# Quarter updates of the down products sent by ScalarE and adding transfers, and chunk 1's up in seven products

## The chip, the core and the metric

The kernel runs on one core of one Trainium2 chip. The engines are TensorE (PE in the profile; PEld is its weight load), VectorE (DVE), ScalarE (ACT), GpSimd (POOL) and SyncE (SP). Weights come from HBM over transfers that SP issues. The metric is the device time of one execution in microseconds, the median over runs.

## What is computed

A decoder trunk over 512 tokens of width 1024, two layers deep. A layer is a half-step feed-forward (FFN), a mixer, and a second half-step feed-forward; the first layer's mixer is a gated linear attention (GLA), the second's a stick-breaking attention (SB). A norm ends the whole.

```python
def swiglu(h, w_gate, w_up, w_down):
    return (jax.nn.silu(h @ w_gate) * (h @ w_up)) @ w_down

# layer i
x += 0.5 * swiglu(rmsnorm(x, ffn1_norm[i]), ...)   # width 1024 -> 2816 -> 1024
x += mixer_i(rmsnorm(x, mix_norm[i]))
x += 0.5 * swiglu(rmsnorm(x, ffn2_norm[i]), ...)
```

So the stages in order are FFN1, GLA, FFN2, FFN3, SB, FFN4. All is in 32-bit floats.

## The kernel before

**Layout.** The state x lies in SBUF as eight tiles `xs[0..7]` of 128 features by 512 tokens. Matmuls run on a rounded format, so each operand is split into a high part (a cast by ACT, L538 for weights, L1261 for data) and a low part (a subtraction by DVE, L539 and L1262), and each 128-row product is three matmuls: high by high, low by high, high by low.

**An FFN stage.** The 2816 inner features are 11 chunks of 256, in five groups: chunk 0; chunks 1 to 3; 4 to 6; 7 to 9; 10 (in the last stage 7 and 8, then 9 and 10). For each chunk come a gate product and an up product, whose product is the inner value; when a group's inner values are there, its down product updates x. A plain gate or up is two features (`feat`, L479) of 24 matmuls of 128x512 each. From chunk 2 on, gate and up use a scheme with seven products instead of eight (`FFN.seven`, L1164): the weight block is cut into quarters, the data in two halves of features by two of tokens, and with sums of quarters and sums of data halves 7 x 12 matmuls of 128x256 do the work. The constants are `SEVEN = 2` for gates and `SEVEN_UP = (2, ..., 10)` for ups. The weight sums (`s12` at L1149 and L1150, `s34` at L1155 and L1156) are DVE's, as are the sums of the normed input (`ts`, L1271, split as `th`, `tl`). The third product of each seven (t3 below, on `s34`) needs all of these. The normed input itself is `xn` (L1255), from x and the scale R, which `rstd_wide` makes at L1019 and L1022.

**The downs.** Groups 1, 2 and 3 have their down in seven products too (`seven_down`), in four parts of two output blocks each, or, for a group of two chunks, in two parts of twice that. In a part the products are, in order: a11 into a PSUM tile `ps_w`, which ACT copies to `ps_z` (L843); t1 into `ps_q`; t2 onto `ps_w`; b21 onto `ps_z`; then t3 onto `ps_w`, b22 onto `ps_q` and t4 onto `ps_w`. For three chunks each is 9 matmuls of 128x256 (L825). After t1, t2, b21, t3, b22 and t4 a quarter of an x tile pair (128 features by 256 tokens) gets half of the running sum added: six updates by DVE (`add`, L831). That of t3 goes by a copy `u3` which ACT takes out of `ps_w` (L869), so that t4 need not wait for DVE. t1 and t3 update the same quarter, and t2 and b22.

**What sets the order.** Program order is not the order on the engines. A `Planner` collects all instructions, prices each by engine, shape and kind, and lists them by dependence, time of readiness and due time, once for each engine; PE's order may pull matmuls ahead out of the next 60. The result is a fixed order on each engine, where an instruction waits at the head of its queue. POOL's instructions stay in program order. Transfers are priced by bytes. So an edit in one place shifts the order around it.

**POOL** has little to do: constants, cleared tiles, and the loads `gr` (L1464), `tri`, `lf`, `negm` (L1959) and `fin` (L2008).

Of the kernel before, what the change touches and what calls it, by code (L numbers as in the profile page):

```python
# [11 lines left out]
F32 = mybir.dt.float32  # L12
# [3 lines left out]
AF = mybir.ActivationFunctionType  # L16
ALU = mybir.AluOpType
PSUM = bass.MemoryType.PSUM

P = 128  # L20
# [409 lines left out]
def turns(t):  # L430

    return t.rearrange("p (two n) -> p n two", two=2)


def flat(ps):

    return ps.rearrange("p (n two) -> p two n", two=2)


def pair(t):  # L440

    return t.rearrange("p (two n) -> p two n", two=2)
# [3 lines left out]
def decoder(ctx: ExitStack, tc: tile.TileContext, a: dict, out: bass.AP):  # L446
    nc = tc.nc
# [28 lines left out]
    xs = [xp.tile([P, T], F32, name=f"x{k}") for k in range(KD)]  # L476
# [311 lines left out]
    def seven_down(pool, w, r0, hs, part, n, per):  # L788

        H = T // 2
        W_ = per * P
        lower, upper = (
            Chunk(w[r0 : r0 + 2 * n * P, c : c + W_].rearrange("(f p) c -> p f c", p=P), 2 * n, W_)
            for c in (part * W_, 512 + part * W_)
        )
        lower.few = upper.few = True
        v = {}

        def halves():

            lo, up = (c.load().rearrange("p (c two) d -> p two c d", two=2) for c in (lower, upper))
            return lo[:, 0], lo[:, 1], up[:, 0], up[:, 1]

        def sums_12(_):
            a11, _, a21, a22 = halves()
            s = v["s12"] = pool().tile([P, 2 * n, W_], F32, tag="s", bufs=4, name="s12")
            nc.vector.tensor_tensor(out=s[:, 0:n], in0=a21, in1=a22, op=ALU.add)
            nc.vector.tensor_tensor(out=s[:, n:], in0=s[:, 0:n], in1=a11, op=ALU.subtract)  # L810
            return s

        def sums_34(_):
            a11, a12, a21, _ = halves()
            s = pool().tile([P, 2 * n, W_], F32, tag="s", bufs=4, name="s34")
            nc.vector.tensor_tensor(out=s[:, 0:n], in0=a11, in1=a21, op=ALU.subtract)
            nc.vector.tensor_tensor(out=s[:, n:], in0=a12, in1=v["s12"][:, n:], op=ALU.subtract)
            return s

        def prod(ps, w, k0, m, b, first):  # L820
            for c in range(n):
                bh, bl = (turns(t) for t in hs[c][b])
                wh, wl = (t[:, k0 + c, m * P : (m + 1) * P] for t in w)
                for i, (l_, r_) in enumerate(((wh, bh), (wl, bh), (wh, bl))):
                    nc.tensor.matmul(  # L825
                        ps, l_, r_, start=first and c + i == 0, stop=c == n - 1 and i == 2, skip_group_check=True
                    )

        def add(m, up, col, ps):
            x = pair(xs[part * per + m + 4 * up][:, col * H : col * H + H])  # L830
            nc.vector.scalar_tensor_tensor(out=x, in0=ps, scalar=0.5, in1=x, op0=ALU.mult, op1=ALU.add)  # L831

        def body_1(W):
            a11, s, v["a2"] = W
            ws, zs, qs = [], [], []
            for m in range(per):
                ws.append(psum("ps_w")[:, 0:H])
                prod(ws[m], a11, 0, m, "b11", True)
            for m in range(per):


                zs.append(psum("ps_z")[:, 0:H])
                nc.scalar.copy(zs[m], ws[m])  # L843
            yield

            ps = psum("ps_q")
            for m in range(per):
                qs.append(ps[:, m * H : (m + 1) * H])
                prod(qs[m], s, 0, m, "t1", m == 0)
            for m in range(per):  # L850
                add(m, 1, 1, flat(qs[m]))
            yield
            for m in range(per):
                prod(ws[m], s, n, m, "t2", False)
                add(m, 0, 1, flat(ws[m]))
            yield
            for m in range(per):
                prod(zs[m], v["a2"], 0, m, "b21", False)
                add(m, 0, 0, flat(zs[m]))
            v["w"], v["q"] = ws, qs  # L860
            yield

        def body_2(W):
            (s,) = W
            ws, qs = v["w"], v["q"]
            for m in range(per):
                prod(ws[m], s, 0, m, "t3", False)
                u3 = pool().tile([P, H], F32, tag="c", bufs=1, name="u3")
                nc.scalar.copy(pair(u3), flat(ws[m]))  # L869
                add(m, 1, 1, pair(u3))  # L870
            yield
            for m in range(per):
                prod(qs[m], s, n, m, "b22", False)
            for m in range(per):
                add(m, 0, 1, flat(qs[m]))
            yield
            for m in range(per):
                prod(ws[m], v["a2"], n, m, "t4", False)
                add(m, 1, 0, flat(ws[m]))
            yield  # L880

        units = [
            (lower, lambda t: halves()[0], n, W_),
            (lower, sums_12, 2 * n, W_),
            (lower, lambda t: halves()[1::2], 2 * n, W_),
        ]
        feed.q.append(Entry(units, body_1))
        feed.q.append(Entry([(lower, sums_34, 2 * n, W_)], body_2))

    def back_tok(w, r0, nf, hs, done):  # L890
# [160 lines left out]
    class FFN:  # L1051
# [8 lines left out]
        NORMED, SEVEN, AHEAD = 6, 2, 2  # L1060
        SEEDED = (0,)
        DOWN_SEVEN = (1, 2, 3)
        SEVEN_UP = (2, 3, 4, 5, 6, 7, 8, 9, 10)

        def __init__(self, wg, wu, wd, gi, nxt, first=False, last=False):
            self.gi, self.normed = gi, False
            if last:
                self.GROUPS = self.LAST_GROUPS
            self.after_ffn = bool(phases) and isinstance(phases[-1], FFN)
            self.defer, self.gates, self.first = [], [], None  # L1070
            self.lead = []
            self.hs = [[] for _ in self.GROUPS]
            base, downs = len(feed.q), []
            self.sums_by = 10**6
            for group, (c0, c1) in enumerate(self.GROUPS):
                slots, put = 2 * (c1 - c0), 0
                for i in range(slots):
                    c, f = c0 + i // 2, i % 2
                    if (c, f) == (self.SEVEN, 0):
                        for put in range(self.AHEAD):  # L1080
                            down(*downs[put], late=put == 0)
                        put = self.AHEAD
                    if f == 0:
                        g, u = Chunk(cols(wg, c * 256, 256), KD, 256), Chunk(cols(wu, c * 256, 256), KD, 256)
                    d = self.defer if i == 0 and c == 0 else None
                    f_ = f
                    if first and c == 0:

                        g, u = (Chunk(cols(w, f * P, P), KD, P) for w in (wg, wu))
                        self.lead += [g, u]  # L1090
                        f_ = 0
                    if c >= self.SEVEN:
                        if f == 0:
                            self.sums_by = min(self.sums_by, len(feed.q) - base)
                            self.seven(g)
                    elif c not in self.SEVEN_UP:
                        feat(g, f_, self.evac_g, defer=d)
                    elif f == 0:
                        feat(g, 0, self.evac_g), feat(g, 1, self.evac_g)
                        self.sums_by = min(self.sums_by, len(feed.q) - base)  # L1100
                    if group - 1 in self.DOWN_SEVEN and f == 0 and c == c0:
                        b0, b1 = self.GROUPS[group - 1]
                        per = 2 if b1 - b0 == 2 else 1
                        args = (lambda: self.tp, wd, b0 * 256, self.hs[group - 1])
                        parts = [(*args, part, b1 - b0, per) for part in range(4 // per)]
                        if group + 1 == len(self.GROUPS) and not last:
                            held = parts.pop()
                        for x in parts:
                            seven_down(*x)
                    if c not in self.SEVEN_UP:  # L1110
                        feat(u, f_, lambda ps, h=group: self.evac_u(ps, h), defer=d)
                    elif f == 1:
                        self.seven(u, group)

                    while c >= self.SEVEN and put < min(len(downs), len(downs) * (i + 1) // 3):
                        down(*downs[put])
                        put += 1
# [9 lines left out]
                if group in self.DOWN_SEVEN:  # L1127
                    downs = []
# [10 lines left out]
        def seven(self, ch, group=None):  # L1139
# [4 lines left out]
            H = T // 2  # L1144
# [58 lines left out]
            def body_2(W):  # L1203
# [1 line left out]
                w, q = (v[n][:, 0:H] for n in "wq")  # L1205
                o0, o1 = v["o"]
                prod(w, s, 0, lambda j: self.t_half(2, j), first=False)
                u3 = self.tp.tile([P, H], F32, tag="c", bufs=1, name="u3")
                nc.scalar.copy(pair(u3), flat(w))
                nc.vector.tensor_tensor(out=o1[:, H:T], in0=u3, in1=o1[:, H:T], op=ALU.add)  # L1210
                yield
# [1149 lines left out]
```

## Time and profile before

| what | value |
|---|---|
| median of 3 runs | 1741.15 us (1739.17 to 1742.62) |
| profiled execution | 1741.74 us, its span 1740.0 us |
| granted TensorE clock | 0.999 |
| PE busy | 1729.9 us, 99%, 13206 matmuls |
| DVE busy | 1618.7 us, 93% |
| ACT busy | 1142.1 us, 66% |
| POOL busy | 10.0 us, 24 instructions |
| moved by transfers | 179.35 MB |

Busy time says which engine is full; the chain of waits says which engine the end depended on. The scale R of FFN2 is ready at 554.6 us and that of FFN4 at 1421.5; FFN3 starts near 880, GLA near 317 and SB near 1164 us.

### The profile page before, as it was taken

How to read it: one execution, taken by the hardware profiler on the slowest of the kernel's cores; microseconds unless marked ns; L12 is line 12 of the kernel's file. 1: busy time of each engine (PE TensorE's matmuls, PEld its weight loads, DVE VectorE, ACT ScalarE, POOL GpSimd, SP SyncE). 2: the span in 40 equal slices, each digit the busy share in tenths (PEclk: the TensorE clock that was granted, in tenths of full speed). 3: DMA queues.
4: the chain of work that ended last, by engine and by line, in shares of the span. 5: the costliest groups of instructions: out<-in, count | busy, mean ns of one | idle time of the engine just before them, and what ended most of it. 6: DMA issues, size and time to landing. Idle time of an engine off the chain costs nothing.

```text
span 1740.0 us, 32878 instructions
## 1 busy us (share of the span) xinstructions
PE 1729.9 (99%) x13206; PEld 1633.0 (94%) x13206; DVE 1618.7 (93%) x2856; ACT 1142.1 (66%) x2056; POOL 10.0 (1%) x24
## 2 busy tenths in 40 slices
PE   9999999999999999999999999999999999999998
PEld 8999999988888999999989999999888888999997
DVE  8999999987888999999999999998898669999997
ACT  7666666664656766666677575657889757666655
POOL 0000000100000000000000000000000000000000
PEclk9999999999999999999999999999999999999999
DMA  6433333321223333333233333233222233333422
GB/s 187 134 101 119 104 116 107 97 95 51 73 98 106 115 106 115 101 119 110 92 115 122 108 112 119 89 105 88 62 73 76 72 106 115 110 110 110 122 87 81
DMA packets 209324, 179.35 MB, mean 103 GB/s; under 512 B 4434, under 2 KB 197252, under 8 KB 209172
## 3 DMA queue, kind: packets, MB, share of 16 engines
q1 hardware_dynamic: 208320, 175.91, 32.8%
q8 instruction: 103, 1.69, 0.4%
q0 software_dynamic: 608, 1.05, 0.2%
q14 instruction: 49, 0.40, 0.1%
q10 hardware_dynamic: 244, 0.29, 0.0%
HBM read 175.17 MB, written 2.10 MB: 102 GB/s over the span
## 4 chain that ended last, share of the span: by engine, by line
PE 91%; DVE 7%; ACT 1%; DMA 1%; issue 1%; DVEq 0%; ACTq 0%; SPq 0%
PE ps_w L1164 21%; PE ps_f L479 15%; PE ps_q L1164 10%; PE ps_w L825 10%; PE ps_q L825 5%; PE ps_z L1164 5%; PE ps_t L479 5%; PE ps_b L479 4%; PE ps_d L479 4%; PE ps_z L825 3%; DVE wl L539 2%; PE ps_z L1849 2%; PE ps_oT L1934 1%; PE ps_T L1919 1%; PE ps_bt L479 1%; PE ps_S L479 1%
## 5 line engine op out<-in xcount | busy, mean ns | idle before, releaser
L538 ACT CAST wh<-s 128x1024 fp32r<-128x1024 f32 (+1 forms) x236 | 229.2, 971 | 113.4 <-PE ps_q L1164 28.1
L539 DVE TENSOR_TENSOR wl<-raw,wh 128x1024 fp32r<-128x1024 f32 x241 | 254.1, 1056 | 31.3 <-ACT wh L538 31.1
L539 DVE TENSOR_TENSOR wl<-s,wh 128x1024 fp32r<-128x1024 f32 (+1 forms) x236 | 263.1, 1115 | 1.6 <-ACT wh L538 1.4
L538 ACT CAST wh<-raw 128x1024 fp32r<-128x1024 f32 x241 | 221.3, 921 | 58.5 <-PE ps_b L479 20.7
L1164 PE MATMUL ps_w<-th,wh 128*128 128x256 f32 x864 | 238.0, 275 | 0.0
L1164 PE MATMUL ps_w<-th,wl 128*128 128x256 f32 x864 | 237.6, 275 | 0.0
L1164 PE MATMUL ps_w<-tl,wh 128*128 128x256 f32 x864 | 237.6, 275 | 0.0
L479 PE MATMUL ps_f<-xh,wh 128*128 128x512 f32 x432 | 166.7, 386 | 0.0
L1164 PEld LDWEIGHTS ps_w<-th,wh 128*128 128x128 f32 x864 | 165.8, 192 | 0.4 <-ACT o L1197 0.2
L1164 PEld LDWEIGHTS ps_w<-tl,wh 128*128 128x128 f32 x864 | 165.9, 192 | 0.0
L1164 PEld LDWEIGHTS ps_w<-th,wl 128*128 128x128 f32 x864 | 165.9, 192 | 0.0
L479 PE MATMUL ps_f<-xh,wl 128*128 128x512 f32 x432 | 163.7, 379 | 0.0
L479 PE MATMUL ps_f<-xl,wh 128*128 128x512 f32 x432 | 163.7, 379 | 0.0
L539 DVE TENSOR_TENSOR wl<-rawd,wh 128x384 fp32r<-128x384 f32 (+2 forms) x152 | 92.6, 614 | 1.1 <-ACT wh L538 1.1
L479 PEld LDWEIGHTS ps_f<-xl,wh 128*128 128x128 f32 x432 | 81.6, 189 | 12.1 <-DVE xl L941 0.2
L479 PEld LDWEIGHTS ps_f<-xh,wh 128*128 128x128 f32 x432 | 81.7, 189 | 11.0
L479 PEld LDWEIGHTS ps_f<-xh,wl 128*128 128x128 f32 x432 | 81.7, 189 | 10.7
L825 PE MATMUL ps_w<-hh,wh 128*128 128x256 f32 x324 | 90.5, 279 | 0.0
L825 PE MATMUL ps_w<-hh,wl 128*128 128x256 f32 x324 | 89.1, 275 | 0.0
L825 PE MATMUL ps_w<-hl,wh 128*128 128x256 f32 x324 | 89.1, 275 | 0.0
L538 ACT CAST wh<-rawd 128x384 fp32r<-128x384 f32 (+2 forms) x152 | 84.6, 566 | 4.1 <-PE ps_f L479 1.8
L1164 PE MATMUL ps_w<-nh,wl 128*128 128x256 f32 x288 | 79.2, 275 | 0.0
(353 smaller groups left out, 5747.2 us busy)
## 6 DMA issues: line engine op xcount, KB each, us to landing
raw<-in_ffn_w_gate_dram SPq DMA_DIRECT2D x43, 1024.0 KB, 5.4
raw<-in_ffn_w_up_dram SPq DMA_DIRECT2D x43, 1024.0 KB, 5.3
rawd<-in_ffn_w_down_dram SPq DMA_DIRECT2D x88, 384.0 KB, 3.5
raw<-in_gla_w_in_dram SPq DMA_DIRECT2D x12, 1024.0 KB, 5.2
rawd<-in_ffn_w_down_dram SPq DMA_DIRECT2D x18, 512.0 KB, 3.7
raw<-in_sb_w_in_dram SPq DMA_DIRECT2D x16, 512.0 KB, 4.0
raw<-in_gla_w_out_dram SPq DMA_DIRECT2D x4, 1024.0 KB, 5.0
raw<-in_sb_w_in_dram SPq DMA_DIRECT2D x4, 1024.0 KB, 5.2
```

The costliest lines, as they stand in the source:

```text
L479: nc.tensor.matmul(ps, l, r, start=first, stop=last, skip_group_check=seeded)
L538: nc.scalar.copy(h[:, k], part)
L539: nc.vector.tensor_tensor(out=l[:, k], in0=part, in1=h[:, k].bitcast(F32), op=ALU.subtract)
L825: nc.tensor.matmul(ps, l_, r_, start=first and c + i == 0, stop=c == n - 1 and i == 2, skip_group_check=True)
L1164: st["pe"] = nc.tensor.matmul(o, l_, r_, start=first and j + n == 0, stop=j == 3 and n == 2, skip_group_check=True).ins
L1849: nc.tensor.matmul(o_, l_, r_, start=first, stop=last, skip_group_check=True)
L1919: nc.tensor.transpose(ps[:, c0 : c0 + P], ys[yb][:, yc + j * P : yc + (j + 1) * P], ident)
L1934: nc.tensor.matmul(po[e * 64 : e * 64 + 64, j * P : T], self.v[j][:, c : c + 64], self.wt[p, e][bk][:, c0 : c0 + n], start=j == 0, stop=j ...
```

## The change

Four of the six quarter updates of `seven_down` (after t2, b21, t3 and t4) are made by a new `send`: ACT writes half of the PSUM block into an SBUF tile `c`, of which there are two in turn, and POOL issues a transfer of 128 KB that adds the tile to the quarter of x. The copy `u3` of `seven_down` goes; the one in `FFN.seven` shares the two tiles. The updates after t1 and b22 stay with DVE. And `SEVEN_UP` takes in chunk 1, in FFN2, FFN3 and FFN4; the first stage's keeps its form. Chunk 1's up in seven products needs all of `ts` before it, so the two down parts that stood ahead of chunk 2 stand ahead of chunk 1's up now, behind its gate's two features.

```diff
--- before.py
+++ after.py
@@ -830,6 +830,11 @@
             x = pair(xs[part * per + m + 4 * up][:, col * H : col * H + H])
             nc.vector.scalar_tensor_tensor(out=x, in0=ps, scalar=0.5, in1=x, op0=ALU.mult, op1=ALU.add)
 
+        def send(m, up, col, ps):
+            t = pool().tile([P, H], F32, tag="c", bufs=2, name="c")
+            nc.scalar.activation(pair(t), ps, AF.Copy, scale=0.5)
+            nc.gpsimd.dma_start(xs[part * per + m + 4 * up][:, col * H : col * H + H], t, accum_op=ALU.add)
+
         def body_1(W):
             a11, s, v["a2"] = W
             ws, zs, qs = [], [], []
@@ -852,11 +857,11 @@
             yield
             for m in range(per):
                 prod(ws[m], s, n, m, "t2", False)
-                add(m, 0, 1, flat(ws[m]))
+                send(m, 0, 1, flat(ws[m]))
             yield
             for m in range(per):
                 prod(zs[m], v["a2"], 0, m, "b21", False)
-                add(m, 0, 0, flat(zs[m]))
+                send(m, 0, 0, flat(zs[m]))
             v["w"], v["q"] = ws, qs
             yield
 
@@ -865,9 +870,7 @@
             ws, qs = v["w"], v["q"]
             for m in range(per):
                 prod(ws[m], s, 0, m, "t3", False)
-                u3 = pool().tile([P, H], F32, tag="c", bufs=1, name="u3")
-                nc.scalar.copy(pair(u3), flat(ws[m]))
-                add(m, 1, 1, pair(u3))
+                send(m, 1, 1, flat(ws[m]))
             yield
             for m in range(per):
                 prod(qs[m], s, n, m, "b22", False)
@@ -876,7 +879,7 @@
             yield
             for m in range(per):
                 prod(ws[m], v["a2"], n, m, "t4", False)
-                add(m, 1, 0, flat(ws[m]))
+                send(m, 1, 0, flat(ws[m]))
             yield
 
         units = [
@@ -1060,12 +1063,14 @@
         NORMED, SEVEN, AHEAD = 6, 2, 2
         SEEDED = (0,)
         DOWN_SEVEN = (1, 2, 3)
-        SEVEN_UP = (2, 3, 4, 5, 6, 7, 8, 9, 10)
+        SEVEN_UP = (1, 2, 3, 4, 5, 6, 7, 8, 9, 10)
 
         def __init__(self, wg, wu, wd, gi, nxt, first=False, last=False):
             self.gi, self.normed = gi, False
             if last:
                 self.GROUPS = self.LAST_GROUPS
+            if first:
+                self.SEVEN_UP = self.SEVEN_UP[1:]
             self.after_ffn = bool(phases) and isinstance(phases[-1], FFN)
             self.defer, self.gates, self.first = [], [], None
             self.lead = []
@@ -1076,7 +1081,7 @@
                 slots, put = 2 * (c1 - c0), 0
                 for i in range(slots):
                     c, f = c0 + i // 2, i % 2
-                    if (c, f) == (self.SEVEN, 0):
+                    if (c, f) == (self.SEVEN, 0) and not put:
                         for put in range(self.AHEAD):
                             down(*downs[put], late=put == 0)
                         put = self.AHEAD
@@ -1097,6 +1102,9 @@
                         feat(g, f_, self.evac_g, defer=d)
                     elif f == 0:
                         feat(g, 0, self.evac_g), feat(g, 1, self.evac_g)
+                        for put in range(self.AHEAD):
+                            down(*downs[put], late=put == 0)
+                        put = self.AHEAD
                         self.sums_by = min(self.sums_by, len(feed.q) - base)
                     if group - 1 in self.DOWN_SEVEN and f == 0 and c == c0:
                         b0, b1 = self.GROUPS[group - 1]
@@ -1205,7 +1213,7 @@
                 w, q = (v[n][:, 0:H] for n in "wq")
                 o0, o1 = v["o"]
                 prod(w, s, 0, lambda j: self.t_half(2, j), first=False)
-                u3 = self.tp.tile([P, H], F32, tag="c", bufs=1, name="u3")
+                u3 = self.tp.tile([P, H], F32, tag="c", bufs=2, name="u3")
                 nc.scalar.copy(pair(u3), flat(w))
                 nc.vector.tensor_tensor(out=o1[:, H:T], in0=u3, in1=o1[:, H:T], op=ALU.add)
                 yield
```

In numbers: 144 matmuls of 128x512 go and 252 of 128x256 come on PE; 192 adds go on DVE; 192 sends come and 48 copies go on ACT; 192 transfers come on POOL. SP's order has the same 254 rows. Line numbers of the new kernel run ahead of the old ones by 5 (L838 to L843 becomes L848) and by 8 from the class `FFN` on (L1262 becomes L1270).

Three places show how the order moves. The first is ACT in one part of the first stage's first seven-product down, before (`wh` are casts of weights, `ps_z<-ps_w` begins a part):

```order
L843 COPY ps_z_1646<-ps_w_1636 128x256
L538 CAST wh_1679<-rawd_1496 128x384
L869 COPY u3_1711<-ps_w_1636 128x256
L538 CAST wh_1683<-s12_1596 128x768
L538 CAST wh_1687<-rawd_1496 128x384
L538 CAST wh_1693<-s34_1633 128x768
L538 CAST wh_1687<-rawd_1594 128x384
L843 COPY ps_z_1747<-ps_w_1737 128x256
```

and the same part now:

```order
L848 COPY ps_z_1658<-ps_w_1648 128x256
L538 CAST wh_1695<-rawd_1500 128x384
L835 ACTIVATE c_1680<-ps_w_1648 128x256
L835 ACTIVATE c_1692<-ps_z_1658 128x256
L538 CAST wh_1699<-s12_1606 128x768
L538 CAST wh_1703<-rawd_1500 128x384
L835 ACTIVATE c_1727<-ps_w_1648 128x256
L538 CAST wh_1709<-s34_1645 128x768
L538 CAST wh_1703<-rawd_1604 128x384
L835 ACTIVATE c_1749<-ps_w_1648 128x256
L848 COPY ps_z_1765<-ps_w_1755 128x256
```

Four sends stand where one copy stood; the third, `c_1727` (t3's), takes the tile of the first, `c_1680` (t2's), with two casts behind it before t4's.

The second is PE in that part, from the end of b22 into t4, before:

```order
L825 MATMUL ps_q_1648<-hh_1287,wl_1591 128x256
L825 MATMUL ps_q_1648<-hl_1288,wh_1590 128x256
L825 MATMUL ps_w_1636<-hh_641,wh_1584 128x256
L825 MATMUL ps_w_1636<-hh_641,wl_1585 128x256
L825 MATMUL ps_w_1636<-hl_642,wh_1584 128x256
```

and now:

```order
L825 MATMUL ps_q_1660<-hh_1287,wl_1601 128x256
L825 MATMUL ps_q_1660<-hl_1288,wh_1600 128x256
L825 MATMUL ps_w_1755<-nh_341,wh_1695 128x256
L825 MATMUL ps_w_1755<-nh_341,wl_1696 128x256
L825 MATMUL ps_w_1755<-nl_342,wh_1695 128x256
L825 MATMUL ps_w_1755<-nh_398,wh_1695 128x256
L825 MATMUL ps_w_1755<-nh_398,wl_1696 128x256
L825 MATMUL ps_w_1648<-hh_641,wh_1594 128x256
L825 MATMUL ps_w_1648<-hh_641,wl_1595 128x256
```

Five matmuls of the next part's a11 (`ps_w_1755`) now stand between b22 and t4.

The third is DVE at the start of FFN2, around the split of `s34` for the first seven products of the stage. Before:

```order
L1262 TENSOR_TENSOR tl_7115<-ts_6758,th_7114 128x512
L1340 TENSOR_TENSOR ts_6925<-t_6845 128x256
L1155 TENSOR_TENSOR s34_6958<-raw_6818 128x512
L1156 TENSOR_TENSOR s34_6958<-raw_6818,s12_6891 128x512
L539 TENSOR_TENSOR wl_6955<-raw_6818,wh_6954 128x1024
L1271 TENSOR_TENSOR ts_6809<-xn_6799,ts_6809 128x256
L539 TENSOR_TENSOR wl_7006<-s34_6958,wh_7005 128x1024
L1262 TENSOR_TENSOR nl_6647<-t_6845,nh_6646 128x256
```

and now:

```order
L1164 TENSOR_TENSOR s34_6943<-raw_6786,s12_6890 128x512
L1270 TENSOR_TENSOR nl_6878<-xn_6871,nh_6877 128x512
L1279 TENSOR_TENSOR ts_6881<-xn_6871,ts_6881 128x256
L1270 TENSOR_TENSOR tl_7104<-ts_6832,th_7103 128x512
L539 TENSOR_TENSOR wl_6995<-s34_6943,wh_6994 128x1024
L1185 TENSOR_TENSOR o0_7045<-ps_z_7044,t_6866 128x256
L1270 TENSOR_TENSOR tl_7108<-ts_6881,th_7107 128x512
L1157 TENSOR_TENSOR s12_6998<-raw_6893 128x512
```

The split `wl_6995<-s34_6943` is now that of chunk 1's up, with the normed input's last pieces (`nl`, `ts`) immediately ahead of it and a split of `ts` (`tl_7108`) behind.

## The prediction

> **What bounds the kernel now.** I read the page first, then PE's waits, then stages by windows, then the chain at the start of a stage.
>
> ```profile
> span 1740.0 us, 32878 instructions
> PE 1729.9 (99%) x13206; PEld 1633.0 (94%) x13206; DVE 1618.7 (93%) x2856; ACT 1142.1 (66%) x2056; POOL 10.0 (1%) x24
> PE 91%; DVE 7%; ACT 1%; DMA 1%; issue 1%; DVEq 0%; ACTq 0%; SPq 0%
> ```
>
> PE is busy 99% of the span and is 91% of the chain: time is matmul count times spacing, plus PE's stalls. Those are small, by the waits of PE's weight loads:
>
> ```profile
> PEld ps_oT L1934 <- issue: 8.8, 40, 0.3
> PEld ps_f L479 <- DVE nl L1262: 0.8, 1, 0.8
> PEld ps_f L479 <- ACT nh L1261: 0.7, 1, 0.7
> PEld ps_q L825 <- DVE wl L539: 0.5, 2, 0.3
> PEld ps_w L825 <- ACT ps_z L843: 0.2, 1, 0.2
> PEld ps_w L825 <- DVE x L831: 0.2, 1, 0.2
> ```
>
> (us in total, times, longest.) The largest lies in the SB mixer, untouched. The two of 0.8 and 0.7 stand at the start of FFN4; the last three are in seven-product downs. So relief for VectorE can return at most 1.5 + 0.9 = 2.4 us, however many of its adds go. The stages differ, though (us; busy time of PE, PEld, DVE, ACT, POOL; clock; DMA share):
>
> ```profile
> 103.00:131.00 28.00, 28.00 (x252) 27.96 (x252) 27.80 (x59) 14.85 (x33) 0.00 (x0) 1.00 0.36 108
> 556.00:597.00 41.00, 41.00 (x192) 35.90 (x191) 41.00 (x70) 29.69 (x49) 0.00 (x0) 1.00 0.31 89
> 884.00:915.00 31.00, 31.00 (x150) 27.27 (x150) 30.96 (x53) 23.17 (x40) 0.00 (x0) 1.00 0.33 95
> 1426.00:1462.00 36.00, 35.31 (x163) 30.29 (x162) 35.99 (x60) 26.17 (x44) 0.00 (x0) 1.00 0.28 81
> ```
>
> The first row is four parts of a seven-product down, the others the starts of FFN2, FFN3 and FFN4. In the starts DVE is full beside a full PE, with no spare time to be early with; in FFN4 PE already loses 0.7. ACT has room in the down: 14.85 of 28.
>
> **The change. Matmuls.** The start of FFN2 in the chain (start, us, work):
>
> ```profile
> 586.90 10.36 PE ps_d L479 x48
> 597.26 1.34 PE ps_w L1164 x12
> 602.61 1.34 PE ps_w L1164 x12
> 605.29 2.68 PE ps_w L1164 x24
> ```
>
> A 512-wide product takes 10.36/48 = 0.216 us, a 256-wide one 2.68/24 = 0.112. Plain, chunk 1's up is 48 of the first, 10.36 us; as seven products 84 of the second, 9.38. Saved 0.98 in each of the three stages FFN2 to FFN4: **−2.95 us**, since PE sets the end there and has nothing else to do in the time.
>
> **The sends.** Of 288 quarter updates 192 leave DVE:
>
> ```profile
> L831 DVE SCALAR_TENSOR_TENSOR x<-ps_w,x x96: 402/414/425, 114.4 to 1687.3; 128x256 f32<-128x256 f32 x96
> L869 ACT COPY u<-ps_w x48: 353/376/378, 116.4 to 1678.3; 128x256 f32<-128x256 f32 x48
> ```
>
> (ns: least, median, most.) DVE loses 192 adds, one every 0.34 us by the step of 256-wide rows below, 65 us in all; but in the downs its time is off PE's path, so of these 65 no more than the 2.4 us above can come back. I count none of it in the downs: their 0.9 are waits for a weight split or a copy that the new order may as well have. ACT gains 192 sends and drops 48 copies: 144 × 0.376 = 54 us, 1.1 us in a part of 7 us (28/4), where it is idle for 3.3. Hidden. What can be dear is a new wait. Tile "c" has two buffers, so t3's send, the third of a part, may not start before t2's, the first, has landed; t4's products wait for t3's send to leave ps_w. Behind the waiting send stand, on ACT, the casts of the next weights, for which PE waits only later. In the new order 32 products lie between t2's last and t4's first, so 33 steps: 33 × 0.1117 = 3.69 us from start to start. The hand-overs:
>
> ```profile
> 119.02 0.28 PE L825 MATMUL ps_w<-nl,wh 128*128 128x256 f32 x1
> 119.34 0.36 ACT L843 COPY ps_z<-ps_w 128x256 f32<-128x256 f32 x1
> 123.16 0.28 PE L825 MATMUL ps_w<-hl,wh 128*128 128x256 f32 x1
> 123.52 0.38 ACT L869 COPY u<-ps_w 128x256 f32<-128x256 f32 x1 [3.40 <-PE ps_w L825]
> ```
>
> PE to ACT 0.32, a copy 0.37, other hand-overs 0.02 to 0.05: 0.32 + 0.37 + 0.05 (issue) + L + 0.04 + 0.37 + 0.05 = 1.20 + L, with L from issue to landing. **PE stalls if L is over 3.69 − 1.20 = 2.49 us**, by the excess, once a part. There are 44 single parts; the first of FFN2, FFN3 and FFN4 have only 29 steps, 3.24 us, and stall from L = 2.04. The last stage's two double parts send eight tiles each through the two buffers: before t4 may start, two landings stand in series, 1.20 + L + 0.46 + L, against at least 60 steps, 6.70 us, so L may be 2.52; I price the two as six places. In all 41 + 3 + 6 = 50.
>
> No accumulating transfer is in this trace; the nearest (last column: median us to landing):
>
> ```profile
> tri<-in_c_tri_dram POOLq DMA_DIRECT2D x1, 64.0 KB, 2.0
> negm<-in_c_neg_dram POOLq DMA_DIRECT2D x1, 32.0 KB, 2.1
> lf<-in_c_lvl_dram POOLq DMA_DIRECT2D x1, 224.0 KB, 2.6
> fin<-in_final_norm_dram POOLq DMA_DIRECT2D x1, 512.0 KB, 4.6
> out_dram<-x SPq DMA_DIRECT2D x2, 128.0 KB, 2.0
> ```
>
> Bounds of L for 128 KB: below, 2.0 (tri; out_dram of the same size). negm to lf is 0.5 us per 192 KB: 2.35 at 128 KB, and 2.68 if the destination, read as well, counts as bytes. Above, fin, which ran beside weight loads: negm to fin is (4.6 − 2.1)/480 = 0.0052 us per KB, so 2.60 at 128 KB and 3.27 with the destination counted. I choose **2.45**, between the two readings of negm and lf, which are of the same queue and nearest in size: no stall in 41 parts, 3 × (2.45 − 2.04) = **+1.2 us** in the three short ones, nothing in the double parts. At 2.68: 50 × 0.19 = +9.5; at 3.27: 50 × 0.78 = +39.
>
> The Trainium skill, "DMA: Bandwidth & Descriptors", section "Anatomy of one DMA — SWDGE (gpsimd) path", fits transfers issued by GpSimd as 2.0 us plus the bytes at 436 KB per us. By it a send would be an estimated 2.3 us, 2.6 if its destination counts, about the same two sides of the threshold; it gives no time for an accumulation, and no run here shows one.
>
> The add that DVE keeps on the same quarter (b22's) waits for t2's landing: b22 ends 27 × 0.1117 = 3.0 us after t2, the send lands 0.32 + 0.37 + 0.05 + 2.45 = 3.2 after. That is 0.2 of DVE's time, out of four adds saved, 1.4: hidden, and if L is 3.27, 1.0, still covered.
>
> **Starts of stages.** Chunk 1's up needs the normed input's sums first, so PE reaches the first third product (t3) of a seven two features, 48 × 0.216 = 10.36 us, sooner: at 602.61 − 10.37 = 592.24 on FFN2's clock. DVE must then have split s34, the second weight sum, with everything that the normed input asks of it done before; the sums and 256-wide pieces of the up come on top. Its rows from the scale R on:
>
> ```profile
> 555.26 1.22 DVE L539 TENSOR_TENSOR wl<-raw,wh 128x1024 fp32r<-128x1024 f32 x1
> 556.39 0.68 DVE L1301 TENSOR_TENSOR t<-ps_f,R 128x512 f32<-128x512 f32 x1
> 557.00 0.68 DVE L1308 TENSOR_TENSOR t<-ps_f,R 128x512 f32<-128x512 f32 x1
> 557.59 0.74 DVE L1255 SCALAR_TENSOR_TENSOR xn<-x,gT,R 128x512 f32<-128x512 f32 x1
> 558.25 0.68 DVE L1309 TENSOR_TENSOR t<-t 128x512 f32<-128x512 f32 x1
> 594.25 0.41 DVE L1271 TENSOR_TENSOR ts<-xn,ts 128x256 f32<-128x256 f32 x1
> 594.59 1.21 DVE L539 TENSOR_TENSOR wl<-s,wh 128x1024 fp32r<-128x1024 f32 x1
> ```
>
> From start to start: 1.13 us for 1024 wide, 0.603 for 512, 0.66 for xn, 0.336 for 256. Before, that split begins at 594.59 and ends 595.72, 6.8 us ahead of PE. In the new order 61 rows stand from 555.26 to its end, 30 of 512, 16 of 256, 8 xn and 7 of 1024: 18.09 + 5.38 + 5.28 + 7.91 = 36.66 (66 rows and 40.46 before), so 591.92, 0.3 us ahead. Counted likewise FFN3 is 0.2 late, FFN4 even. FFN4, 0.65 ahead before by that count, still lost 1.5, since ACT's casts wait on DVE too. I take 0.6 a stage, **+1.8 us** (bounds 0 and 1.5, so 0 to 4.5), and 0.6 of FFN4's old 1.5 back, **−0.6**, for its work is now in another order.
>
> **POOL's queue.** It runs in program order, so the mixers' loads now stand behind the sends:
>
> ```profile
> 50.99 1.04 POOL L1464 DMA_DIRECT2D gr<-in_gla_w_in_dram  x1 [49.67 <-DVE ts L1271]
> 312.95 0.95 POOL L1466 MEMSET gs<- 128x1024 f32 x1 [260.92 <-ACT wh L538]
> ```
>
> gr now starts behind FFN1's last send, near 310, still before the memset that stood at 313; it landed in 5.0 us and is read near 343. Hidden; its cost without that cover would be a few us, once.
>
> Sum on the profiled run, 1741.74 (span 1740.0, 0.6 over the median): −2.95 + 1.2 + 1.8 − 0.6 = −0.55. On the median of 1741.15: **1740.6 us, no change that a measurement tells** (0.2%, 3.5 us).
>
> **Rivals.**
> - All in time, 0.25. L stays under 2.04, DVE's relief carries the starts, and the old stalls go: −2.95 − 1.5 − 0.9 = −5.3, **1736 us**. For it: out_dram's 2.0 and DVE's 65 us less. Against: the starts hold no adds to lose.
> - The send becomes the bound, 0.16: every landing slower than 2.49. It costs 50 × (L − 2.49) and tells from L = 2.57 on: at 2.68 1740.6 + 9.5 = **1750 us**, at 3.27 **1780**. For it: bytes read twice, and the nearness of 2.45 to 2.49. Against: negm to lf.
> - Only sends that meet a load are late, 0.12: the DMA share is 0.36 in the downs, so 0.36 × 0.78 × 50 = +14, **1755 us**. For it fin's 4.6 beside loads; against it tri's 2.0. The Trainium skill, "DMA: Bandwidth & Descriptors", section "Queues, rings and completion order", has each DMA engine serve its queues in turn, packet by packet, which is this mechanism; the trace shows it only by fin.
> - The starts are late by their upper bound, 0.10: 3 × 1.5 in place of 1.8 and nothing back, 1740.6 + 2.7 + 0.6 = **1744 us**; half of this chance I put above 1744.6, since that bound is FFN4's loss at a margin of 0.65, and the new margins are smaller. Against it: what DVE still does before that split could be put behind it in part.
>
> **The numbers.** Forecast 0.37. Faster by over 0.2% (under 1737.7): the first rival and 0.02 of the forecast's edge, 0.27. Slower (over 1744.6): 0.16 + 0.12 + 0.05 of the fourth, 0.33. The rest is 0.40. The likeliest's own range is 1738 to 1744. For 8 in 10 it goes from 1735.5 past the case of 1755 to 1757; left out are sends of L over 2.8 in all places and a gain beyond all old stalls.
>
> **What would show it.** On the trace after: 1392 512-wide ps_f products in place of 1536 and spacing unchanged; the landing of the c transfers against 2.49; waits of ps_w at the downs' products for ACT's copy out of ps_w, 0.4 us in three first parts and none elsewhere; waits for s34's split at the starts of about 0.6. Wrong if the sends' median landing is over 2.57 or PE's stalls at the starts sum to over 5 us.

## The result and the profile after

The changed kernel takes 1865.12 us (1861.62 to 1871.42 in 4 runs) where the kernel before takes 1740.16 beside it: a ratio of 1.072, with a 95% interval of 1.0688 to 1.0752. The forecast was 1740.6 us with a range up to 1757. The change loses 125 us.

The page of the kernel after, its first lines, its chain and its groups of the sends:

```profile
span 1859.8 us, 33635 instructions
PE 1764.6 (95%) x13314; PEld 1657.4 (89%) x13314; DVE 1587.1 (85%) x2694; ACT 1198.8 (64%) x2218; POOL 175.6 (9%) x216
...
PE 23%; issue 21%; POOL 3%; DMA 2%; DVE 2%; ACT 1%; POOLq 0%; DVEq 0%; ACTq 0%
...
L836 POOL DMA_DIRECT2D x<-c x192 | 165.7, 876 | 1542.7 <-ACT c L835 1360.6
...
L835 ACT ACTIVATE c<-ps_w 128x256 f32<-128x256 f32 x144 | 55.4, 385 | 161.7 <-DMA x<-c 131.0
...
x<-c POOLq DMA_DIRECT2D x192, 128.0 KB, 3.2
```

PE is no longer full (95%), VectorE neither (85% in place of 93%), and ScalarE sat idle for 161.7 us ahead of its sends out of ps_w, 131 of it until a transfer had landed. The last row is the number that the prediction had to guess: a send lands 3.2 us after its issue in the median.

PE's waits in the kernel after, in the first fence, and ScalarE's, in the second (us in total, times, longest):

```profile
PEld ps_w L825 <- ACT c L835: 62.2, 51, 4.3
PEld ps_w L1172 <- ACT ps_z L1199: 24.0, 6, 5.1
PEld ps_w L825 <- ACT ps_z L848: 13.3, 11, 2.0
...
PEld ps_w L1172 <- DVE wl L539: 0.5, 2, 0.4
```
```profile
ACT c L835 <- DMA x<-c: 169.7, 99, 5.8
```

Of 192 sends 99 had to wait for the landing of an earlier one, 169.7 us in all: 59.4 us ahead of t3's sends, 49.7 ahead of t4's, 38.7 of b21's and 21.9 of t2's. PE lost 99.5 us behind ScalarE. 62.2 of it are waits for sends: 52.5 at the place that the prediction named (t4 behind t3's send, 44 times), 9.7 where t3 waited for t2's send (7 times). The other 37.3 are waits for copies out of ps_w at the start of the next product, a part's (L848) or a gate's or up's (L1199); 16 of these 17 copies stood in ScalarE's queue behind a send that waited for a landing. One such place in the timeline, PE and ScalarE:

```profile
1148.27 0.28 PE L825 MATMUL ps_w<-hl,wh 128*128 128x256 f32 x1
...
1153.93 0.38 ACT L835 ACTIVATE c<-ps_w 128x256 f32<-128x256 f32 x1 [5.77 <-DMA x<-c]
1154.22 1.04 ACT L538 CAST wh<-s 128x1024 fp32r<-128x1024 f32 x1
...
1155.15 0.38 ACT L1199 COPY ps_z<-ps_w 128x256 f32<-128x256 f32 x1
...
1155.58 0.41 PE L1172 MATMUL ps_w<-th,wh 128*128 128x256 f32 x1 [4.91 <-ACT ps_z L1199]
1155.79 0.41 PE L1172 MATMUL ps_w<-th,wl 128*128 128x256 f32 x1
1156.00 0.42 PE L1172 MATMUL ps_w<-tl,wh 128*128 128x256 f32 x1
```

The send of t4 waits 5.77 us for its tile. Behind it stand a cast and the copy L1199, which has nothing to do with sends; PE waits 4.91 us for that copy. And then its matmuls follow each other every 0.21 us where 0.112 is their spacing. The windows of that stretch say why (the column behind POOL's is the granted clock):

```profile
1147.00:1149.00 2.00, 1.72 (x15) 1.73 (x16) 1.57 (x3) 1.16 (x2) 1.60 (x2) 1.00 0.70 162
1155.50:1158.00 2.50, 2.42 (x12) 2.42 (x13) 2.50 (x4) 0.84 (x3) 0.00 (x0) 0.56 0.36 52
1159.00:1169.00 10.00, 10.00 (x90) 10.00 (x90) 9.01 (x16) 5.95 (x11) 0.00 (x0) 0.99 0.35 107
```

The granted clock is 0.56 over the first 2.5 us after the idle time.

**Where the 119.8 us of span are.** Worked out from the starts of PE's matmuls in both traces, by how much later the next one starts than is usual for its kind:

```
excess over the usual distance    before          after
over 0.15 us (waits)               8.1 us         103.8 us
0.10 to 0.15 us                    8.5            34.5
matmuls saved                                     -2.9
```

So +95.7 us are waits, and +26.0 lateness by 0.10 to 0.15 us, most of it half clock: 11 of the 12 waits of over 2 us are followed, within a few us, by 13 to 26 matmuls at twice their spacing, 190 in all, and there the granted clock stands at 0.5 for 3.4 us, twice for 6.8. The last 1 us lies in smaller differences.

### The profile page after: what moved, and what is told of

It reads as the page before. It is cut to its first block, busy times and chain, and to the rows that moved or that the text cites. A ratio compares the mean times of both kernels' runs of the same rounds, so it can differ in the third digit from the quotient of the medians.

```text
span 1859.8 us, 33635 instructions
## 1 busy us (share of the span) xinstructions
PE 1764.6 (95%) x13314; PEld 1657.4 (89%) x13314; DVE 1587.1 (85%) x2694; ACT 1198.8 (64%) x2218; POOL 175.6 (9%) x216
## 4 chain that ended last, share of the span: by engine, by line
PE 23%; issue 21%; POOL 3%; DMA 2%; DVE 2%; ACT 1%; POOLq 0%; DVEq 0%; ACTq 0%
PE ps_f L479 6%; PE ps_w L1172 3%; POOL x L836 3%; PE ps_t L479 2%; PE ps_b L479 2%; DMA x<-c 2%; PE ps_q L1172 2%; PE ps_z L1857 1%; PE ps_d L479 1%; PE ps_oT L1942 1%; PE ps_z L1172 1%; PE ps_T L1927 1%; PE ps_bt L479 1%; DVE wl L539 1%; PE ps_w L825 1%
## 5 line engine op out<-in xcount | busy, mean ns | idle before, releaser
L539 DVE TENSOR_TENSOR wl<-s,wh 128x1024 fp32r<-128x1024 f32 (+1 forms) x242 | 271.2, 1121 | 75.5 <-ACT wh L538 74.7
L836 POOL DMA_DIRECT2D x<-c x192 | 165.7, 876 | 1542.7 <-ACT c L835 1360.6
L1172 PE MATMUL ps_w<-th,wh 128*128 128x256 f32 x900 | 251.7, 280 | 22.9 <-ACT ps_z L1199 22.9
L1172 PE MATMUL ps_w<-th,wl 128*128 128x256 f32 x900 | 250.3, 278 | 0.0
L1172 PE MATMUL ps_w<-tl,wh 128*128 128x256 f32 x900 | 250.3, 278 | 0.0
L1172 PEld LDWEIGHTS ps_w<-th,wh 128*128 128x128 f32 x900 | 175.2, 195 | 24.3 <-ACT ps_z L1199 24.0
L1172 PEld LDWEIGHTS ps_w<-th,wl 128*128 128x128 f32 x900 | 175.3, 195 | 0.2 <-DVE wl L539 0.2
L1172 PEld LDWEIGHTS ps_w<-tl,wh 128*128 128x128 f32 x900 | 175.3, 195 | 0.0
L835 ACT ACTIVATE c<-ps_w 128x256 f32<-128x256 f32 x144 | 55.4, 385 | 161.7 <-DMA x<-c 131.0
L825 PEld LDWEIGHTS ps_w<-hh,wh 128*128 128x128 f32 x324 | 62.9, 194 | 75.9 <-ACT c L835 62.2
L539 DVE TENSOR_TENSOR wl<-rawd,wh 128x384 fp32r<-128x384 f32 (+2 forms) x152 | 92.0, 617 | 15.4 <-ACT wh L538 15.3
```

Source lines behind the costliest of these rows:

```text
L539: nc.vector.tensor_tensor(out=l[:, k], in0=part, in1=h[:, k].bitcast(F32), op=ALU.subtract)
L825: nc.tensor.matmul(ps, l_, r_, start=first and c + i == 0, stop=c == n - 1 and i == 2, skip_group_check=True)
L835: nc.scalar.activation(pair(t), ps, AF.Copy, scale=0.5)
L836: nc.gpsimd.dma_start(xs[part * per + m + 4 * up][:, col * H : col * H + H], t, accum_op=ALU.add)
L1172: st["pe"] = nc.tensor.matmul(o, l_, r_, start=first and j + n == 0, stop=j == 3 and n == 2, skip_group_check=True).ins
```

## The experiments

The 125 us were first divided between the parts of the change, then the sends' loss between its possible causes. The kernel before, run beside each set of them, took 1739.82 to 1741.14 us.

### One part at a time

`up_only` keeps the old updates and takes the change of the up:

```diff
-        SEVEN_UP = (2, 3, 4, 5, 6, 7, 8, 9, 10)
+        SEVEN_UP = (1, 2, 3, 4, 5, 6, 7, 8, 9, 10)
```

> Chunk 1's up in seven products alone, no sends. Theory A (the loss is the sends: a send's tile is free only when its transfer has landed, 2.67 us where no load runs and up to 7.5 us beside weight loads, and ACT waits for it in order): the three starts save 2.9 us and give back 0 to 1.8, so 1737 to 1740 us. Rival B (the fuller starts of stages cost as well): over 1745 us.

1760.49 us, ratio 1.011 (1.0096 to 1.0124): 19.4 us slower, where 2.9 were to be saved. Rival B holds so far: the up costs too. But little of it is at the starts of the stages, where PE's waits in seven products are 0.2, 3.1 and 0.4 us in the first 60 us or so. Most of its new waits are in the downs, PE's in the first fence, and one of ScalarE's in the second:

```profile
PEld ps_w L825 <- ACT u L869: 7.1, 9, 1.0
...
PEld ps_q L825 <- DVE wl L539: 6.1, 14, 0.8
```
```profile
ACT u L869 <- DVE o L1215: 27.9, 9, 3.3
```

PE waits for VectorE's splits, and for the copy u3 (named `u` here). Ahead of eight of these nine waits ScalarE could not make that copy before VectorE's add at L1215 had emptied the tile c, of which `up_only` has one, as the kernel before has, where the change has two.

The windows of FFN2, FFN3 and most of FFN4, in the first fence of the kernel before, in the second of `up_only`:

```profile
555.00:873.00 318.00, 317.91 (x2565) 309.24 (x2564) 315.11 (x560) 208.48 (x373) 0.00 (x0) 1.00 0.35 106
873.00:1160.00 287.00, 286.99 (x2389) 281.60 (x2389) 285.45 (x512) 186.29 (x343) 0.00 (x0) 1.00 0.37 111
1422.00:1700.00 278.00, 277.26 (x2299) 271.23 (x2298) 274.39 (x491) 179.50 (x326) 0.54 (x1) 1.00 0.34 104
```
```profile
554.00:880.00 326.00, 321.77 (x2608) 311.90 (x2607) 321.25 (x572) 211.28 (x380) 0.00 (x0) 1.00 0.34 104
880.00:1171.00 291.00, 287.13 (x2414) 281.47 (x2414) 289.72 (x519) 189.94 (x348) 0.00 (x0) 1.00 0.36 110
1434.00:1715.00 281.00, 276.86 (x2311) 270.56 (x2309) 277.56 (x498) 179.48 (x328) 0.54 (x1) 1.00 0.34 102
```

The third busy column is VectorE: 315.11 of 318, 285.45 of 287, 274.39 of 278 before. Over whole stages it is nearly as full as PE, with 1.5 to 3.6 us left. The up gives it 5.6 us more in each (1635.5 us of work in all, in place of 1618.7). By the starts of R (554.6, 873.2 and 1421.5 us, and the end at 1740.0, before; 554.1, 880.0, 1434.3 and 1758.2 in `up_only`) the stretches that begin with FFN2, FFN3 and FFN4 grow by 7.3, 6.0 and 5.5 us.

`sends_only` has the sends and the old `SEVEN_UP`:

> The four sends alone, chunk 1's up as before. Theory A: the loss is all here, 1862 to 1872 us. Rival B: under 1850 us, the rest being with the up.

1842.50 us, ratio 1.0607 (1.0572 to 1.0642), 101.4 us slower and under the 1850 of Rival B: most of the loss is the sends', not all of it. The two parts alone sum to 120.8, the whole change to 125: they hardly help or hinder each other, though VectorE, which the up fills further, is the engine that the sends relieve. That a relieved VectorE is of no use where ScalarE waits is a reading that no run tests.

### Transfers or ScalarE's work?

`u_add` keeps the four extractions by ScalarE and lets VectorE add the tile:

```diff
-            nc.gpsimd.dma_start(xs[...][:, col * H : col * H + H], t, accum_op=ALU.add)
+            x = pair(xs[...][:, col * H : col * H + H])
+            nc.vector.tensor_tensor(out=x, in0=pair(t), in1=x, op=ALU.add)
```

> Full change, but each tile c is added to x by VectorE in place of the adding transfer: ACT's four extractions per part stay, the transfers go. Theory A: with no landing to wait for, 1737 to 1746 us. Rival C (ACT's added work in its queue delays the weight casts, with or without transfers): over 1790 us.

1766.67 us, ratio 1.0151 (1.0137 to 1.0165). That is over the 1746 of Theory A, which had not known of the up's loss, and far under Rival C's 1790. Beside `up_only` (1760.49, with one tile c) the extractions into two tiles cost 6 us; beside the change (1865) the transfers cost 98.

`two_late` sends only what t3 and t4 give:

```diff
-                send(m, 0, 1, flat(ws[m]))
+                add(m, 0, 1, flat(ws[m]))
...
-                send(m, 0, 0, flat(zs[m]))
+                add(m, 0, 0, flat(zs[m]))
```

> Full change, but only t3's and t4's updates are sent; t2's and b21's stay VectorE adds. A tile c then comes round once a part, about 7 us after its last send, and no add of VectorE in the same part waits for a send. Theory A: landings beyond 6 us are rare, so nearly all of the 125 us comes back: 1738 to 1755 us. Rival D (the transfers themselves disturb the loads or PE, in proportion to their number): about half comes back, near 1800 us.

1746.50 us, ratio 1.0033 (1.0021 to 1.0046), inside Theory A's range. Half of the sends in place of all gives back 119 of 125 us, though their landings are no shorter:

```profile
x<-c POOLq DMA_DIRECT2D x96, 128.0 KB, 3.2
```

So the loss does not go by the number of transfers. It goes by how soon a tile is wanted again: ScalarE waits for landings here for only 3.4 us.

```profile
ACT c L835 <- DMA x<-c: 3.4, 6, 1.3
```

`late_only` is `two_late` with the old up:

> Sends for t3 and t4 alone, with chunk 1's up as before the change. In two_late the up's saving of 2.9 us went under in waits for VectorE (the up adds 5.7 us to it in each of three stages). If VectorE's load is what two_late lost by: 1737 to 1741 us, at least 5 below two_late. If the two sends cost by themselves: 1743 us or more.

1747.17 us, ratio 1.0037 (1.0025 to 1.0050): the two sends alone cost 6 us, and the up added nothing to that. Both kernels have 96 adds less on VectorE; that this is why the up is free here is argued, not shown.

### The tiles, and the order

`six_tiles`:

```diff
-            t = pool().tile([P, H], F32, tag="c", bufs=2, name="c")
+            t = pool().tile([P, H], F32, tag="c", bufs=6, name="c")
...
-                self.t = st["few"].tile([...], F32, tag="rawd", bufs=3, name="rawd")
+                self.t = st["few"].tile([...], F32, tag="rawd", bufs=2, name="rawd")
```

> Full change with six tiles c in turn in place of two; the weight tiles rawd of the downs are two in place of three, to make the room. Theory A (ACT waits for a tile's landing, in order, and PE behind it): the wait goes, and most of the 125 us with it, 1742 to 1765 us, the landings staying as long as they were (median 3.2 us). Rival D (the transfers as such slow loads and engines): over 1800 us. Fewer rawd tiles could add a few us to either.

1788.80 us, ratio 1.0289 (1.0270 to 1.0307). It comes between the two: 76 of the 125 us are back, 48 are left. The wait that Theory A names is gone altogether, though the landings are longer (median 3.75 us): no send of ScalarE's waits for a landing, in place of 99, and PE's waits behind sends are 15.3 us in place of 62.2.

```profile
PEld ps_w L825 <- ACT c L835: 15.3, 28, 1.6
```

Its control has the two rawd tiles alone, in the kernel before:

> The kernel before with two tiles rawd in place of three and no sends: the control to six_tiles, which lost 48 us with two rawd tiles and six tiles c. If the fewer rawd tiles made that loss: 1770 us or more. If the sends did: under 1750 us.

1768.54 us, ratio 1.0159 (1.0144 to 1.0175): 28.7 us for a third of the rawd tiles, between the two bounds again. If the costs add, the sends cost some 20 us with six tiles against 125 with two. What of these 20 is the up's (19.4 alone) was not separated. Two of VectorE's waits in `six_tiles` show what is left:

```profile
DVE s L809 <- DMA rawd<-in_ffn_w_down_dram: 20.1, 23, 2.5
DVE x L831 <- DMA x<-c: 16.5, 12, 3.0
```

The first is for weights of the downs, which have a tile less; the second is the add that VectorE keeps (b22's), waiting for t2's landing.

`price5` leaves two tiles, and changes what the planner counts for a send:

```diff
-            return 2050.0 + total / 318.0, total / 318.0
+            return (2050.0 + total / 318.0 if e != "Pool" else 5000.0), total / 318.0
```

> Full change with two tiles, but the planner counts 5.0 us for a transfer of POOL's in place of 2.46, so that it writes its orders for late landings. Theory E (the wait is an error of the order, which was written for 2.46 us): most comes back, under 1775 us. Theory A alone (two tiles are too few whatever the order: four sends of 3.6 us mean in pairs take over 7 us, a part's length): some comes back, 1790 to 1850 us.

1812.33 us, ratio 1.0409 (1.0392 to 1.0427). Theory E falls: with an order for late landings 53 us come back and 72 stay. But these 72 are not the old wait:

```profile
ACT c L835 <- DMA x<-c: 26.4, 27, 3.3
```

ScalarE waits 26.4 us for landings ahead of sends, in place of 169.7. PE's waits behind ScalarE's sends, copies and casts and behind VectorE are now many and short, none over 3.0 us. So the order decides where the lateness is paid; that two tiles cost this much under any order is not shown.

### What a landing is made of

`plain_pool` copies in place of adding, so it leaves the update out; `plain_act` does the same from ScalarE's queue:

```diff
-            nc.gpsimd.dma_start(..., t, accum_op=ALU.add)
+            nc.gpsimd.dma_start(..., t)
```

> Full change, but POOL's transfers copy the tile c over the quarter of x and add nothing (the update is left out). If the addition is what makes a landing 2.67 us where no load runs: 2.3 us or less, and some 1770 to 1800 us in all. If it is the way of any transfer of POOL's: 2.6 us or more, longest again over 6, and within 20 us of the change.

> As plain_pool (a copy over the quarter in place of the addition), but issued by ScalarE's queue. Theory F: where no load runs some 1.9 us, and still about 4 us at load shares of 0.4 to 0.8, time near plain_pool's 1800 us. If POOL's way of making descriptors is what is slow beside loads: under 2.5 us at all shares, and 1740 to 1760 us.

`plain_pool` took 1800.51 us and `plain_act` 1816.98 (one run each). Their landings without a load came as the first branch of each expectation said (below); the times lie at its upper edge and 17 us above `plain_pool`'s. Four fences follow: the DMA row of `plain_pool`, that of `plain_act` (the change's stands above), and the issuing instruction by its line, in the change and in `plain_pool` (ns: least, median, most):

```profile
x<-c POOLq DMA_DIRECT2D x192, 128.0 KB, 2.9
```
```profile
x<-c ACTq DMA_DIRECT2D x192, 128.0 KB, 2.6
```
```profile
L836 POOL DMA_DIRECT2D x<-c x192: 851/860/1197, 113.7 to 1806.4; - x192
```
```profile
L836 POOL DMA_DIRECT2D x<-c x192: 538/538/678, 113.5 to 1745.3; - x192
```

Sorting the sends by what share of the 16 DMA engines weight loads took beside them (from 0.9 us behind the issue to the landing), worked out from the packets of each trace (medians in the first two columns; of `plain_act` the trace has 170 landings):

```
                 no load (share under 0.05)    share 0.4 and over    mean of all
change           2.69 us (76 sends)            4.92 us (57)          3.71 us
plain_pool       1.97 us (82)                  3.95 us (74)          3.04 us
plain_act        1.99 us (71)                  4.19 us (62)          3.06 us
down_loads_once  2.68 us (134)                 4.94 us (34)          3.25 us
```

The addition costs 0.7 us a send, 0.32 of it already in the issue. The greater part of the lateness comes with loads: some 2 us, for a plain copy as well. `plain_act` lands as early and as late as `plain_pool` does, so the long landings aren't POOL's way of making descriptors. It was slower than `plain_pool` although its landings are alike. Each issue takes 0.47 us of ScalarE, whose queue is the one PE waits for; that this is the reason is likely and was not tested.

Does the load beside a send make it late, or does it only come at the same time? `half_loads` was the first try:

```diff
-                        g, u = Chunk(cols(wg, c * 256, 256), KD, 256), Chunk(cols(wu, c * 256, 256), KD, 256)
+                        g = u = Chunk(cols(wg, c * 256, 256), KD, 256)
```

> Full change, but gate and up of a chunk work on one loaded block (the up's weights are the gate's), so 42 of 84 loads of 1 MB go, and with them a good half of the traffic outside the downs. Theory F (a landing is longer the more loads lie in the rings beside it: 2.69 us at a share under 0.05, 4.7 to 5.1 at 0.4 to 0.8): fewer sends are late, time 1790 to 1845 us, the landings by share as before. If something else than loads makes the long landings: within 15 us of 1865.

1857.6 us, median landing 3.1: within 15 us of the change, which its expectation gave to "something else". But 56 of its sends still had a load share of 0.4 and over, against 57 in the change: the gate and up loads which it removes hardly run beside sends. So it says nothing on either theory. `down_loads_once` removes those that do:

```diff
+        if part == 0:
+            st["shared_down"] = [Chunk(...) for c in (part * W_, 512 + part * W_)]
+        lower, upper = st["shared_down"]
```

> Full change, but the four parts of a down work on the first part's weights, so that three quarters of the down loads (rawd) go; gate and up loads stay. (half_loads took away loads that hardly run beside the sends, and its landings stayed.) Theory F (the sends' long landings are those beside the down loads): the median landing falls from 3.2 to about 2.7 us, and the time to 1760 to 1815 us. If the loads don't matter: within 15 us of 1865.

1798.39 us (one run), inside Theory F's range, and its transfers:

```profile
x<-c POOLq DMA_DIRECT2D x192, 128.0 KB, 2.7
```

With three quarters of the down loads gone, 67 of 125 us come back and the median is that of sends without a load. The 34 sends that still meet loads are as late as before. So the down loads beside the sends are the cause of most of the long landings. And 2.69 us without any load is still too long for two tiles:

```profile
ACT c L838 <- DMA x<-c: 103.4, 72, 3.7
```

Of ScalarE's waits for landings in this run 54, together 66.9 us, are for sends with a share under 0.05.

### Giving VectorE back its time

The last three tried whether a smaller form wins. `two_late_price` is `two_late` with 5.0 us counted for a send and 0.7 us more for a load; `t3_send_up` sends only t3's update, `t3_send_only` the same without the up.

> two_late (t3's and t4's updates sent, chunk 1's up in seven products) with orders written for 5.0 us per send and 0.7 us more per load than the planner counts, since loads land later beside sends. If two_late's 5 us over the kernel before are errors of the order: 1736 to 1742 us. If they are VectorE's and ScalarE's want of time: 1744 us or more.

> Of the sends only t3's is left (it takes the place of a copy by ScalarE and an add by VectorE), with chunk 1's up in seven products and the orders written for 5.0 us a send and 0.7 us more a load. Theory G (VectorE is as full as PE in FFN2 to FFN4, idle 0.9 to 3 us of some 300, so that the up's 5.7 us more on it in each of them, 17 us in all, come out as time: up_only's 19 us): the send takes 48 adds of 0.34 us off it, 16 us, VectorE is where it was, and the time is 1737 to 1743 us. If up_only's loss has another cause: over 1750 us.

> As t3_send_up, with chunk 1's up as before the change: VectorE has 16 us less to do and PE the same matmuls. Theory G with PE as the bound as well: 1736 to 1741 us, since there are only 2.4 us of waits to win. If VectorE alone set the time: 1730 us or less.

In this order: 1742.32 us, ratio 1.0013 (1.0004 to 1.0022); 1743.01 us, 1.0013 (1.0004 to 1.0022); 1740.07 us, 0.9997 (0.9988 to 1.0006). `two_late_price` falls between its two bounds: 2.5 us over the kernel before, where `two_late` was 5.4 over, so about half of that was the order's. `t3_send_up` is at the upper edge of Theory G's range, 17 us under `up_only`: with 16 us taken off VectorE the up's loss is nearly gone. That fits VectorE's fullness, but does not show it alone, since `t3_send_up` differs from `up_only` also in its second tile c and in the prices of its order; `up_only` with these two was not run. In FFN2 and FFN3 of `t3_send_up`:

```profile
552.00:871.00 319.00, 318.10 (x2602) 310.18 (x2601) 316.90 (x559) 210.14 (x379) 10.34 (x12) 1.00 0.38 112
871.00:1160.00 289.00, 287.87 (x2424) 282.84 (x2423) 287.72 (x512) 189.17 (x348) 9.46 (x11) 1.00 0.40 115
```

VectorE is nearly where it was before the change, 1.3 to 2.1 us short of full, and PE is 0.9 and 1.1 us short of full, where it was 0.1 and 0.0 short before: the 2.9 us that the up saves are given back in such waits. `t3_send_only` relieves VectorE and gains nothing that the measurement tells, as PE was the bound already. None of the runs beats the kernel before.

## Why the prediction was wrong

- **The count of matmuls** (−2.95 us) was right: the changed kernel's usual spacings sum to 2.9 us less.
- **The landing, L = 2.45 us**, is the term that failed first. It was chosen between two readings of copies from HBM, with the addition left out of account: without loads it is 2.69, nearly the rival's 2.68, at which the sum said 1750. The median is 3.2, near the upper end of 3.27, at which it said 1780. It was taken from rows (negm and lf) beside which no load ran, while the sends run in a stretch whose DMA share was quoted as 0.36. The down loads that make much of this share are the cause, as `down_loads_once` shows. The rival of sends that meet a load had this mechanism, with 3.27 us where 4.92 was measured.
- **"By the excess, once a part"** failed as well, and this is why even the right L gives too little: 50 × (3.71 − 2.49) = 61 us by the mean. At the place that this term prices, t4 behind t3's send, PE waited 52.5 us, so there the term is about right once it has the measured L. But the waits are 95.7 us in all, with most of 26 us of half clock on top. The tiles were followed only from t2 to t3. All four sends of a part go through two tiles: each tile serves twice a part, and a turn takes 0.38 us of ScalarE plus the landing, by estimate 2 × (0.38 + 3.71) = 8.2 us, in a part of 7. So the lateness goes on from send to send: 110.3 of the 169.7 us that ScalarE waited for landings are ahead of sends other than t3's. With two sends a part a turn has 7 us, and the loss is 6 us; with one it has 14, and no send waits.
- **"Behind the waiting send stand, on ACT, the casts of the next weights, for which PE waits only later"** failed. The copies of the next products stand there too, and PE waited 37.3 us for those.
- **The waits of stage starts** (+1.8 us) did not come in the whole change: PE's waits for weight splits in seven products are 0.5 us in all (the last row of its PE waits above). What failed here is a term at nothing: the up's 5.6 us of VectorE's work a stage were followed at the starts only, as if they were free behind them. `up_only` loses 19.4 us, most of it behind the starts, with 17 us more on a VectorE that is about 99% full through these stages. The profile showed that in the quoted row of the down, 27.80 of 28.00 us, which was used for ScalarE's room only. How the 19.4 divide between VectorE's fullness, the one tile c and the order stays open.
- **The add that VectorE keeps** (b22's) waited for t2's landing 14 times, 18.7 us in all; it is hidden, as forecast, for none of PE's waits in the changed kernel is for it.
- **POOL's queue** was right: no wait on the loads that moved behind the sends stands among PE's.
- **The half clock** was in no term. The Trainium skill, "TensorE: Matmul & The Clock Gate", section "What's actually happening", has the clock halve after an idle window of about 3.4 us and come back after as long a busy one. The trace agrees with the second length (0.5 for 3.4 or 6.8 us). For the first, waits of 2.3 us were long enough here, and one of 3.0 was not.

## What to carry to other kernels

A buffer that a transfer must free is a resource with a rate: count its turns per stretch of work (here two turns of some 4.1 us in 7 us), with landings taken from the loaded stretch where the transfer will run, and not only the distance to its first reuse. A wait put into an in-order queue delays all that stands behind it, so list those instructions by who waits for them. Before counting a saving on the fullest engine, sum the second fullest over the whole stage: here that one was at about 99%, and 17 us of work added to it came with 19.4 us of time.

## What was not expected of the hardware

A transfer of 128 KB between places of SBUF landed, by the medians, in 1.97 us as a copy and 2.69 as an addition where loads had under 0.05 of the DMA engines, and in 3.95 and 4.92 us where they had 0.4 and more; the longest took 7.5. Its issue takes POOL 0.54 us as a copy and 0.86 as an addition. After 11 of 12 waits of over 2 us PE's matmuls came at half rate for some 3 to 5 us; from 1155.5 to 1158 us the granted clock was 0.56.
